# Up-projection of a decoder MLP: grouping the wide and the narrow products of a k-tile

## The chip, the cores and the metric

The kernel runs on one core of one Trainium2 chip. The metric is the device time of one execution in microseconds; for runs of the same kernel the median is taken. TensorE does the matrix products, VectorE (DVE) and ScalarE (ACT) prepare the weights and empty the accumulators, and the DMA queues of SyncE bring the weights from the chip's memory.

## The reference

Two consecutive decoder layers work on 256 tokens of width 2048, in float32. Each has a mixer (mLSTM heads and sliding-window attention) and an MLP with a squared ReLU; both are wrapped in RMSNorms whose shift, scale and gate come from a projection of a conditioning vector. The change is in the first product of the MLP:

```python
def squared_relu_mlp(h, w_up, w_down):
    return jnp.square(jax.nn.relu(h @ w_up)) @ w_down

def reference(...):
    for l in range(DEPTH):
        ...
        y = token_mixer(h, ...)
        x = x + gate_a * rms_norm(y, g_post_mix[l])
        h = rms_norm(x, g_pre_mlp[l]) * (1.0 + scale_m) + shift_m
        y = squared_relu_mlp(h, w_up[l], w_down[l])   # 2048 -> 8192 -> 2048
        x = x + gate_m * rms_norm(y, g_post_mlp[l])
```

## The kernel before

**Products in two parts.** Each float32 operand is split into a high part, rounded to the fp32r format, and a low part, the remainder, so that a product of two operands is made of three fp32r products: high x high, low x high and high x low. Weights arrive in tiles `raw` of 128 x 2048; `split` (line 227) makes from each half of such a tile a slab of two k-tiles: `whi` on ACT (L236) and `wlo` on DVE (L240). Four slabs of each kind are held, and `prefill` splits up to three ahead. In layer 0 and part of layer 1 DVE also works through the conditioning weights (`ada_op`, L208).

**Units.** A `Unit` is one block of 512 output columns over all its k-tiles of 128. `Unit.mm` calls its body once for each k-tile of a slab. There are several bodies:

- `body_xs` (L336) makes tokens the rows of the result: the weights stream past, 512 columns in each product. It is used for the down-projection (`dn`), the mixer's output (`op`) and up unit 0.
- `body_ws` (L341) makes weight columns the rows: the 256 tokens stream past, 256 columns in each product (`qa`, `qm`, `km`, and some up units).
- `body_wide` (L347) does the same for most up units, but streams the high and low tokens together: one product of 512 columns (`whi` with high and low tokens, L352) and one of 256 (`wlo` with the high tokens, L353). Each of the four groups of 128 weight columns has a PSUM bank of its own, `u.ps[j]`; the first half of the bank takes high x high and low-weight x high, the second half high-weight x low tokens. The 512-column product of the first k-tile starts the accumulation of the bank, the 256-column product of the last k-tile ends it.

With `body_wide` go the up units 4 to 15 of layer 0 and 2 to 15 of layer 1: 26 units of 16 k-tiles, with 4 products of each kind in a k-tile. Every product has its own load of 128 x 128 weights into the array (PEld in the profile).

**Order of the MLP.** Units are done in an order written out by hand: for each e from 0 to 7, up unit 2e + 2, then the four down units (e, c), then up unit 2e + 3. For e = 7 there is no further up unit, so the down units (7, c) come straight after up unit 15. A down unit (e, c) has 8 k-tiles, the first four from up unit 2e and the other four from 2e + 1.

**Banks.** There are two pools of four PSUM banks. Up units with an odd number (and unit 2) take the four banks of the pool `ps_x`, the others those of `ps_mm`; down units with c < 2 (from e = 1) take two of `ps_x`, the others two of `ps_mm`.

**Emptying.** `evac_up_wide` (L1056) goes over the four banks in two pairs. For a pair, ACT copies the second halves (L1063), DVE adds the first halves (L1065), after which the banks are free; then come the squared ReLU (L1068), the high part (L1069) and the low part (L1070) of the result, from which the down-projection reads.

**Order on the engines.** The instructions of an engine run in the order in which the program lists them. The framework that builds the program sorts instructions of one engine by priority and by what is ready by its own estimate, so that it can differ at single places from the order in which the code issues them.

Of the kernel before, what the change touches and what calls it, by code (L numbers as in the profile page):

```python
# [16 lines left out]
P = 128  # L17
D = 2048
KT = D // P
S = 256  # L20
# [19 lines left out]
def hymba_kernel(ctx: ExitStack, tc: tile.TileContext, x_d, c_d, cols_d, cons_d, wada_d,  # L40
                 wst_d, wsu_d, win_d, wg_d, wout_d, wup_d, wdn_d, out_d):
    nc = tc.nc
    V, A, T, G = nc.vector, nc.scalar, nc.tensor, nc.gpsimd
# [303 lines left out]
    def body_wide(u, xh, xl, wh, wl, kt):  # L347


        for j in range(4):  # L350
            cs = slice(j * P, (j + 1) * P)
            T.matmul(u.ps[j], wh[:, cs], u.act.both(kt), start=kt == 0, stop=False, skip_group_check=True)  # L352
            T.matmul(u.ps[j][:, 0:S], wl[:, cs], xh, start=False, stop=kt == u.nk - 1, skip_group_check=True)  # L353

    def body_mix(u, xh, xl, wh, wl, kt):
        for j in range(2):
# [183 lines left out]
    for l in range(DEPTH):  # L540
# [564 lines left out]
        def up(u):  # L1105

            un = Unit(f"up{L}_{u}", ("up", l, u), KT, hT2, body_wide, u % 2 == 1 or u == 2, 4)
            un.run()
            tups[u] = Task(evac_up_wide(un, u))
# [150 lines left out]
```

## Time and profile before

| | |
|---|---|
| time, median of 3 runs | 2243.57 us (2241.97 to 2245.36) |
| the profiled execution: time | 2245.62 us |
| the profiled execution: span | 2243.8 us |
| mean granted TensorE clock | 0.984 |
| TensorE busy (PE) | 2158.0 us, 96% |
| weight loads (PEld) | 1842.4 us, 82% |
| VectorE busy | 1719.7 us, 77% |
| ScalarE busy | 1097.5 us, 49% |
| mean DMA rate | 263 GB/s |

How to read it: each matmul row names its line and has the form output <- stationary or moving tiles, the array's rows and columns, the moving operand's shape, and the count. After the bar stand the total busy time, the mean duration of one instruction, and the idle time of the engine just before such instructions, with what ended it. Matmuls overlap each other in the array, so the duration of one is longer than the distance between the starts of two; the chain that ended last, in order of time, gives the distance. A line such as L333 belongs to a helper used by many units; the names of the tiles tell which unit it is (`up`, `dn`, `qa`).

### The profile page before, as it was taken

How to read it: one execution, taken by the hardware profiler on the slowest of the kernel's cores; microseconds unless marked ns; L12 is line 12 of the kernel's file. 1: busy time of each engine (PE TensorE's matmuls, PEld its weight loads, DVE VectorE, ACT ScalarE, POOL GpSimd, SP SyncE). 2: the span in 40 equal slices, each digit the busy share in tenths (PEclk: the TensorE clock that was granted, in tenths of full speed). 3: DMA queues.
4: the chain of work that ended last, by engine and by line, in shares of the span. 5: the costliest groups of instructions: out<-in, count | busy, mean ns of one | idle time of the engine just before them, and what ended most of it. 6: DMA issues, size and time to landing. Idle time of an engine off the chain costs nothing.

```text
span 2243.8 us, 29891 instructions
## 1 busy us (share of the span) xinstructions
PE 2158.0 (96%) x11658; PEld 1842.4 (82%) x11658; DVE 1719.7 (77%) x2386; ACT 1097.5 (49%) x1585; POOL 1.4 (0%) x14
## 2 busy tenths in 40 slices
PE   6789999899999999999989999989999999999998
PEld 5679777698888888888869988778888888888886
DVE  7989999688888888888577898957666767555557
ACT  4246753645444444434465566556443444444433
POOL 0000000000000000000000000000000000000000
PEclk9999999899999999999989999999999999999999
DMA  9998689498889888888539866745666667655551
GB/s 371 385 361 301 235 303 351 161 355 315 319 305 338 306 332 316 318 315 317 192 118 337 317 227 243 269 164 204 228 225 233 229 226 263 210 188 190 186 191 71
DMA packets 82351, 589.88 MB, mean 263 GB/s; under 512 B 9185, under 2 KB 9633, under 8 KB 10785
## 3 DMA queue, kind: packets, MB, share of 16 engines
q1 hardware_dynamic: 82210, 587.98, 71.7%
q8 instruction: 91, 1.49, 0.3%
q14 instruction: 50, 0.41, 0.1%
HBM read 585.81 MB, written 2.13 MB: 262 GB/s over the span
## 4 chain that ended last, share of the span: by engine, by line
PE 84%; DVE 10%; ACT 3%; issue 2%; DMA 1%; SPq 0%; DVEq 0%; ACTq 0%
PE dn L333 31%; PE up L352 17%; PE up L353 9%; PE up L333 6%; PE op L333 5%; DVE raw L208 4%; PE om L333 3%; PE vm L333 2%; PE qa L333 2%; DVE wlo L240 2%; PE qm L333 2%; PE km L333 2%; PE kva L333 1%; DVE x L400 1%; DMA raw<-in_wout_dram 1%
## 5 line engine op out<-in xcount | busy, mean ns | idle before, releaser
L240 DVE TENSOR_TENSOR wlo<-raw,whi 128x1024 fp32r<-128x1024 f32 x720 | 875.8, 1222 | 433.0 <-ACT whi L236 431.3
L236 ACT ACTIVATE whi<-raw 128x1024 fp32r<-128x1024 f32 x720 | 759.3, 1059 | 872.3 <-PE dn L333 344.2
L352 PE MATMUL up<-htm,whi 128*128 128x512 f32 x1664 | 588.3, 399 | 0.0
L353 PE MATMUL up<-htm,wlo 128*128 128x256 f32 x1664 | 467.5, 281 | 0.0
L208 DVE SCALAR_TENSOR_TENSOR raw<-raw,cact 128x2048 f32<-128x2048 f32 x192 | 437.2, 2284 | 7.1 <-DMA raw<-in_wada_dram 7.1
L333 PE MATMUL dn<-whi,sh 128*128 128x512 f32 x1024 | 399.5, 390 | 0.0
L333 PE MATMUL dn<-wlo,sh 128*128 128x512 f32 x1024 | 399.0, 390 | 0.0
L333 PE MATMUL dn<-whi,sl 128*128 128x512 f32 x1024 | 398.9, 390 | 0.0
L352 PEld LDWEIGHTS up<-htm,whi 128*128 128x128 f32 x1664 | 313.2, 188 | 77.1
L353 PEld LDWEIGHTS up<-htm,wlo 128*128 128x128 f32 x1664 | 314.6, 189 | 0.6
L333 PEld LDWEIGHTS dn<-whi,sh 128*128 128x128 f32 x1024 | 192.3, 188 | 40.6 <-DVE r L1065 0.4
L333 PEld LDWEIGHTS dn<-wlo,sh 128*128 128x128 f32 x1024 | 192.3, 188 | 40.2
L333 PEld LDWEIGHTS dn<-whi,sl 128*128 128x128 f32 x1024 | 192.4, 188 | 39.4 <-DVE sl L1087 0.2
L333 PE MATMUL op<-whi,ct 128*128 128x512 f32 x512 | 164.0, 401 | 2.6 <-ACT whi L236 1.8
L333 PE MATMUL vm<-whi,hta 128*128 128x512 f32 x256 | 90.9, 438 | 30.1 <-ACT whi L236 18.6
L333 PEld LDWEIGHTS op<-whi,ct 128*128 128x128 f32 x512 | 97.6, 192 | 25.2 <-ACT whi L236 2.7
L333 PE MATMUL op<-wlo,ct 128*128 128x512 f32 x256 | 101.3, 401 | 2.1 <-DVE wlo L240 2.0
L333 PE MATMUL qa<-hta,whi 128*128 128x256 f32 x512 | 93.6, 285 | 0.0
L333 PE MATMUL up<-htm,whi 128*128 128x256 f32 x512 | 92.8, 284 | 0.0
L333 PEld LDWEIGHTS vm<-whi,hta 128*128 128x128 f32 x256 | 51.5, 209 | 45.1 <-ACT whi L236 20.1
L333 PE MATMUL om<-whi,hta 128*128 128x512 f32 x256 | 82.3, 401 | 0.0
L333 PEld LDWEIGHTS up<-htm,whi 128*128 128x128 f32 x512 | 80.3, 192 | 0.5
(260 smaller groups left out, 2319.2 us busy)
## 6 DMA issues: line engine op xcount, KB each, us to landing
raw<-in_wada_dram SPq DMA_DIRECT2D x192, 1024.0 KB, 6.5
raw<-in_wdn_dram SPq DMA_DIRECT2D x128, 1024.0 KB, 4.9
raw<-in_wup_dram SPq DMA_DIRECT2D x120, 1024.0 KB, 5.1
raw<-in_win_dram SPq DMA_DIRECT2D x56, 1024.0 KB, 5.5
raw<-in_wout_dram SPq DMA_DIRECT2D x32, 1024.0 KB, 6.3
raw<-in_wst_dram SPq DMA_DIRECT2D x16, 1024.0 KB, 7.3
raw<-in_wsu_dram SPq DMA_DIRECT2D x8, 1024.0 KB, 6.3
gp<-gdr SPq DMA_DIRECT2D x4, 1024.0 KB, 5.7
```

What stands on the lines that cost most here:

```text
L208: V.scalar_tensor_tensor(w, w, 1.0, cact, ALU.mult, ALU.mult, accum_out=modc[l][:, v, j:j + 1])
L236: A.activation(hi, raw, AF.Copy)
L240: V.tensor_tensor(lo, raw, hi.bitcast(F32), ALU.subtract)
L333: T.matmul(o, a, w, start=not self.started[b], stop=last and i == 2, skip_group_check=True)
L352: T.matmul(u.ps[j], wh[:, cs], u.act.both(kt), start=kt == 0, stop=False, skip_group_check=True)
L353: T.matmul(u.ps[j][:, 0:S], wl[:, cs], xh, start=False, stop=kt == u.nk - 1, skip_group_check=True)
L400: V.scalar_tensor_tensor(xc, self.yg[c][tok], r, xc, ALU.mult, ALU.add)
```

## The change

In `body_wide` the loop over the four groups of weight columns is cut in two. The first loop does the four 512-column products of the k-tile, one in each of the four banks; the second does the four 256-column products, in the same order of the banks. The products themselves, their operands, their banks and their start and stop flags are the same. In the code before, the order in a k-tile was wide, narrow, wide, narrow and so on, the two of a bank directly behind each other.

```diff
     def body_wide(u, xh, xl, wh, wl, kt):
 
+        cs = [slice(j * P, (j + 1) * P) for j in range(4)]
         for j in range(4):
-            cs = slice(j * P, (j + 1) * P)
-            T.matmul(u.ps[j], wh[:, cs], u.act.both(kt), start=kt == 0, stop=False, skip_group_check=True)
-            T.matmul(u.ps[j][:, 0:S], wl[:, cs], xh, start=False, stop=kt == u.nk - 1, skip_group_check=True)
+            T.matmul(u.ps[j], wh[:, cs[j]], u.act.both(kt), start=kt == 0, stop=False, skip_group_check=True)
+        for j in range(4):
+            T.matmul(u.ps[j][:, 0:S], wl[:, cs[j]], xh, start=False, stop=kt == u.nk - 1, skip_group_check=True)
```

## The prediction, made before the changed kernel was built or run

> **What bounds the kernel now.** I read the page first: the engine shares, the chain that ended last, and the groups of the two lines that the change moves.
>
> ```profile
> PE 2158.0 (96%) x11658; PEld 1842.4 (82%) x11658; DVE 1719.7 (77%) x2386; ACT 1097.5 (49%) x1585; POOL 1.4 (0%) x14
> PE dn L333 31%; PE up L352 17%; PE up L353 9%; PE up L333 6%; PE op L333 5%; DVE raw L208 4%; PE om L333 3%; PE vm L333 2%; PE qa L333 2%; DVE wlo L240 2%; PE qm L333 2%; PE km L333 2%; PE kva L333 1%; DVE x L400 1%; DMA raw<-in_wout_dram 1%
> ...
> L352 PE MATMUL up<-htm,whi 128*128 128x512 f32 x1664 | 588.3, 399 | 0.0
> L353 PE MATMUL up<-htm,wlo 128*128 128x256 f32 x1664 | 467.5, 281 | 0.0
> ```
>
> TensorE bounds the kernel. The two moved lines carry 17% and 9% of the chain, about 580 us. Their idle time is 0.0, so nothing that they wait for can be saved: only their pace, or a new wait, can move the time. The mean durations (399 and 281 ns) are no price, because neighbours overlap; the price is the distance from one start to the next. Next, busy time by stage, for two units of up-projection in layer 1 (the window, its length, busy us of PE, PEld, DVE, ACT and POOL, the granted clock, DMA share and GB/s).
>
> ```profile
> 1633.60:1678.40 44.80, 44.80 (x256) 38.89 (x255) 27.65 (x29) 20.31 (x25) 0.00 (x0) 1.00 0.67 233
> ```
>
> PE is busy for the whole stretch at a granted clock of 1.00; DVE, ACT and the DMA have room. Last, the chain in order of time, for the pace of long runs and of the alternation.
>
> ```profile
> 1211.56 25.92 PE qa L333 x216
> 1590.03 43.58 PE dn L333 x192
> 1678.82 43.58 PE dn L333 x192
> ...
> 1640.31 0.23 PE up L352
> 1640.54 0.12 PE up L353
> ```
>
> The dn products stream 512 columns, the qa ones 256 (body_xs and body_ws). A run of 512-column products has one every 43.58 / 192 = 227 ns; a run of 256-column ones every 25.92 / 216 = 120 ns. A pair would be 347 ns at these paces. Between the two dn rows lie two up units, 2 x 64 pairs: (1678.82 - 1590.03 - 43.58) / 128 = 353.2 ns a pair. The alternation thus costs some 6 ns a pair more than the same work in long runs: that is all the change can win, 4 x 6.5 = 26 ns a k-tile, 10.8 us over 26 units x 16 k-tiles.
>
> **The change part by part.** *1. The pace.* Nothing is added or removed: 26 x 16 x 8 = 3328 matmuls, each with its weight load, change order on PE alone; no DMA and no instruction of another engine moves past a queue. A k-tile has 8 changes of width now and 2 afterwards, but a run of four is short. In layer 0, up unit 0 (512 columns, in runs of 12) and units 1 to 3 (256 columns, in runs of 72) take turns, and show how a run settles (256 columns up to 481.79, 512 from 481.91, 256 from 484.66; first column the start in us, x2 two neighbours of one line):
>
> ```profile
> 481.79 0.28 PE L333 MATMUL up<-htm,wlo 128*128 128x256 f32 x1
> 481.91 0.63 PE L333 MATMUL up<-whi,htm 128*128 128x512 f32 x2
> 482.38 0.39 PE L333 MATMUL up<-wlo,htm 128*128 128x512 f32 x1
> 482.61 0.62 PE L333 MATMUL up<-whi,htm 128*128 128x512 f32 x2
> 483.07 0.39 PE L333 MATMUL up<-wlo,htm 128*128 128x512 f32 x1
> ...
> 484.66 0.40 PE L333 MATMUL up<-htm,whi 128*128 128x256 f32 x2
> ...
> 485.01 0.40 PE L333 MATMUL up<-htm,whi 128*128 128x256 f32 x2
> ```
>
> The first three 512-column distances take 482.61 - 481.91 = 0.70 us, the next two 0.46, so four take 0.93 us against 4 x 0.227 = 0.908. Four 256-column ones take 485.01 - 484.66 + 0.12 = 0.47 us, a little under 0.48. A k-tile is then 1.40 us against 4 x 353.2 = 1.413. I take 1.401, a gain of 12 ns. It is the value nearest to the new pattern, since it is what a run of four does after a run of the other width. The bounds: 1.387 where a group settles at once (gain 26 ns), and, on the side of a loss, the 512-column products that follow an alternation:
>
> ```profile
> 1678.65 0.40 PE L333 MATMUL dn<-whi,sh 128*128 128x512 f32 x1
> ...
> 1679.60 0.39 PE L333 MATMUL dn<-whi,sl 128*128 128x512 f32 x1
> ...
> 1681.21 0.39 PE L333 MATMUL dn<-wlo,sh 128*128 128x512 f32 x1
> ```
>
> Here the first four take 1679.60 - 1678.65 = 0.95 us: 0.95 + 0.47 = 1.42 us a k-tile, 8 ns worse than now.
>
> One unit, the first of layer 0, already has the good pace:
>
> ```profile
> 575.90 0.23 PE up L352
> ...
> 579.72 0.23 PE up L352
> ```
>
> Eleven pairs in 3.82 us are 347 ns a pair, in the same order of instructions as elsewhere. The excess is thus no fixed price of a change of width; the pattern can lock in more than one way, which is why I keep both bounds. This unit would lose 16 x 14 ns = 0.2 us. The other 25 x 16 = 400 k-tiles gain 400 x 12 ns = 4.8 us.
>
> *2. Entering the down-projection.* After the alternation, eleven dn products take 1681.21 - 1678.65 = 2.56 us, against 11 x 0.227 = 2.497: 0.063 us lost. After a run of 256s five take 483.07 - 481.91 = 1.16 against 1.133, 0.027 lost. The difference, 0.036 us, at the 12 such places whose entry has no other wait: 0.4 us gained.
>
> *3. The end of a unit.* The four banks now finish 0.35 us apart; afterwards 0.12 us. Bank 0 is complete 0.70 us later relative to the unit's end. At two places, before the last down-projection of each layer (e = 7), the next unit takes exactly the banks that unit 15 just filled:
>
> ```profile
> 1103.45 0.28 PE L353 MATMUL up<-htm,wlo 128*128 128x256 f32 x1
> 1103.77 1.10 ACT L1063 ACTIVATE r<-up 128x256 f32<-128x256 f32 x3 [0.83 <-PE up L353]
> 1104.18 1.14 DVE L1065 TENSOR_TENSOR r<-up,r 128x256 f32<-128x256 f32 x3
> 1104.51 0.28 PE L353 MATMUL up<-htm,wlo 128*128 128x256 f32 x1
> 1104.66 0.19 PEld L333 LDWEIGHTS dn<-whi,sh 128*128 128x128 f32 x1 [0.19 <-DVE r L1065]
> ```
>
> The last product for bank 0 starts at 1103.45, then ACT copies, DVE adds, and only then the dn load starts. From that product to the unit's end it is 1104.63 - 1103.45 = 1.18 us now and 4 x 0.12 = 0.48 afterwards. The wait grows by 0.70 us, twice: 1.4 us lost. Behind the waiting load all of PE is queued. The other 24 unit ends have a whole up or down unit (48 x 0.227 = 10.9 us or more) before their banks or their result are needed, and PE's loads wait at none of them in layer 1's MLP, by the waits from its first unit to its last:
>
> ```profile
> PEld dn L333 <- DVE r L1065: 0.2, 1, 0.2
> ACT whi L236 <- PE up L352: 152.9, 89, 1.9
> ```
>
> ACT's first copy is later there too, by up to 0.70 us, with the splits of weights queued behind it. By the second row these splits wait 152.9 / 89 = 1.7 us each for PE to free a buffer, so ACT is ahead by more than it loses. That buffer is also freed 0.36 us earlier (4 x 0.12 instead of 0.12 before the slab's end), and the low half of the weights is needed 0.68 us later (after four 227 ns products instead of one). Neither ends a wait of PE; both cost nothing.
>
> *4. The start of the first wide unit in layer 0.* Its fourth bank is still being copied out:
>
> ```profile
> 572.16 0.39 PE L352 MATMUL up<-htm,whi 128*128 128x512 f32 x1
> ...
> 573.12 0.59 ACT L1114 ACTIVATE ys<-dn 128x512 f32<-128x512 f32 x1
> 573.56 0.71 PE L352 MATMUL up<-htm,whi 128*128 128x512 f32 x2
> ```
>
> The copy ends at 573.12 + 0.59 = 573.71; the build puts the fourth product off by a k-tile today, so that two 512-column ones (x2) stand in a row. In the new order it would be due at 572.16 + 3 x 0.227 = 572.84, so 0 to 0.9 us is lost, according to how far it is put off again. I take 0.3, nearer the low end, because the build moved it today.
>
> *Sum*: -4.8 + 0.2 - 0.4 + 1.4 + 0.3 = -3.3 us. The profiled execution took 2245.62 us (span 2243.8), so 2242.3 for it; it lies 2.0 above the median of the runs, 2243.57, and from that the forecast is 2240.3, 0.15% faster.
>
> **A rule of the skill.** The distance between products in the rows is 227 and 120 ns in runs, and 353 ns for a pair of both. The Trainium skill, "TensorE: Matmul & The Clock Gate", section "Back-to-back issue gap", makes an isolated gap N / 2.4 + 2.5 ns, whatever stands beside it; that estimate is 216 and 109 ns, 325 ns a pair in either order. By it the pace would gain nothing; the trace disagrees, with 353 against 347 ns for the same columns. It is the first rival below.
>
> **The rivals.** *The order is indifferent*: what a change of width costs grows with the length of the run, so that two changes with runs of four lose as much as eight with runs of one; or the build puts the products back into pairs, as it moved some at 573.56. For it: the longer runs do pay 0.02 us on settling. Against it: the rows at 481.91. Only terms 3 and 4 are left, 1.7 us: 2245.3, or 2243.6 with the pairs back. *The groups settle at once*, as the unit at 575.90 did: 400 x 26 ns = 10.4 us, with terms 2 to 4 (0.4 gained, 1.7 lost) 9.1 gained, 2234.5. For it: that unit lost nothing on four times as many changes of width. Against it: the 0.93 us. *The groups never settle*: four 512s take 0.95 us again and again as after the alternation. 400 x 8 ns = 3.2 us lost, with terms 3 and 4 (1.7) 4.9: 2248.5, slower. It decides from a k-tile of 1.413 + 0.007 us upwards. For it: the rows at 1678.65. Against it: those follow an alternation, which is no longer there.
>
> **How the numbers follow.** About 0.2% (4.5 us) is what a measurement of this kernel can tell from no change: faster means under 2239.1, slower over 2248.1. Forecast, 0.53: 2240.3, own range 2237.5 to 2243, of which 0.15 lies below 2239.1. Settling at once or nearly, 2234 to 2237.5: 0.20, all faster. Order indifferent: 0.17, all same. Never settling: 0.10, of which 0.08 slower. That is faster 0.35, same 0.57, slower 0.08. The range leaves out about a tenth at each end: 2235.5 to 2246.5.
>
> **What would show it.** In the changed kernel the chain between two dn rows should have eight products per k-tile in 1.40 us, (distance of two dn rows less 43.58) / 32. That is 44.8 us for two units, against 45.21. Within a k-tile the 512s should start 0.23 apart, the first ones more, and the 256s 0.12. PE's load of dn should wait on the DVE add about 0.9 us, once in each layer, and ACT's wait for the up product at L1063 should grow by 0.7 us a time. The prediction is wrong if a k-tile takes 1.387 or 1.42 us, if PE waits at other unit ends, or if the products stand in pairs again.

## The result and the profile after

| | before | after |
|---|---|---|
| median of the runs | 2243.65 us (2241.29 to 2246.63) | 2248.49 us (2240.55 to 2250.25) |
| ratio after / before | | 1.0015, 95% interval 1.0008 to 1.0021 |
| the profiled execution: time / span | 2245.62 / 2243.8 us | 2248.9 / 2247.1 us |

The changed kernel is slower by 0.15%. The forecast was 0.15% faster, and 2248.5 us lies above the range. The pace of the products became what was forecast, and its gain is in the trace; two places gave back more than it.

First the page of the changed kernel: shares of the engines, and the groups of the moved lines (L354 is the 256-column product now) and of the down-projection.

```profile
PE 2156.1 (96%) x11658; PEld 1842.7 (82%) x11658; DVE 1718.6 (76%) x2386; ACT 1093.2 (49%) x1585; POOL 1.4 (0%) x14
...
L352 PE MATMUL up<-htm,whi 128*128 128x512 f32 x1664 | 454.2, 394 | 0.0
L333 PE MATMUL dn<-whi,sh 128*128 128x512 f32 x1024 | 400.0, 391 | 4.5 <-DVE r L1066 4.5
L354 PE MATMUL up<-htm,wlo 128*128 128x256 f32 x1664 | 264.8, 281 | 0.0
```

PE is 1.9 us less busy while the span is 3.3 us longer. The moved lines still wait for nothing. The line that the change did not touch, the first product of the down-projection, now has 4.5 us of idle time ahead of it, put down to the DVE add that empties unit 15 (L1066 now, L1065 before).

The pace, from the chain in order of time in layer 1 (start, length, what, count):

```profile
1591.55 43.55 PE dn L333 x192
1679.97 43.57 PE dn L333 x192
...
1635.09 0.91 PE up L352 x4
1636.00 0.47 PE up L354 x4
1636.47 0.93 PE up L352 x4
1637.40 0.47 PE up L354 x4
```

Between two dn blocks lie two units of 16 k-tiles: (1679.97 - 1591.55 - 43.55) / 32 = 1.402 us a k-tile, where before it was 1.413 (4 x 353.2 ns); four wide products take 0.91 to 0.93 us, four narrow ones 0.47.

The entry of dn(7, 0) in layer 0, from the timeline; ahead of it stand unit 15's last narrow products (x4), and in the bracket is the idle time of the engine, of the weight load (PEld) and of the product (PE):

```profile
1101.73 0.63 PE L354 MATMUL up<-htm,wlo 128*128 128x256 f32 x4
...
1101.93 1.06 ACT L236 ACTIVATE whi<-raw 128x1024 fp32r<-128x1024 f32 x1 [1.75 <-PE up L352]
1102.90 1.19 ACT L1064 ACTIVATE r<-up 128x256 f32<-128x256 f32 x4
1103.02 1.23 DVE L240 TENSOR_TENSOR wlo<-raw,whi 128x1024 fp32r<-128x1024 f32 x1 [1.58 <-ACT whi L236]
1104.16 1.08 DVE L1066 TENSOR_TENSOR r<-up,r 128x256 f32<-128x256 f32 x3
...
1104.64 0.19 PEld L333 LDWEIGHTS dn<-whi,sh 128*128 128x128 f32 x1 [2.48 <-DVE r L1066]
1104.64 0.50 PE L333 MATMUL dn<-whi,sh 128*128 128x512 f32 x1 [2.27 <-DVE r L1066]
1104.97 0.39 PE L333 MATMUL dn<-whi,sl 128*128 128x512 f32 x1
...
1105.65 0.62 PE L333 MATMUL dn<-whi,sl 128*128 128x512 f32 x1
...
1106.07 0.63 PE L333 MATMUL dn<-wlo,sh 128*128 128x512 f32 x1
```

Read it from the end. PE waits 2.27 us, for the adds that start at 1104.16. DVE is late because it is busy with `wlo` until about then, and that `wlo` belongs to a split whose `whi` ACT began at 1101.93, ahead of unit 15's copies (1102.90). In the kernel before, three copies stood ahead of that split in ACT's queue: the copies start at 1103.77 (a row in the prediction), and the `whi` follows them:

```profile
1104.76 1.05 ACT L236 ACTIVATE whi<-raw 128x1024 fp32r<-128x1024 f32 x1
```

The order of the two queues has changed, though the diff touches neither engine. The last wide product, which frees the buffer for that split, is now issued before the first bank is complete; that the builder's sorting by readiness put the split first for this reason is inferred from the two orders.

The second reading is the spacing after the wait: 0.33 and 0.23 us first, then 0.42 us from 1105.65 on. The windows show why (window, its length, busy us of PE, PEld, DVE, ACT, POOL; the granted clock is the third number from the end). First the changed kernel in both layers, then the kernel before:

```profile
1105.50:1109.00 3.50, 3.50 (x10) 2.77 (x9) 2.66 (x5) 1.34 (x3) 0.00 (x0) 0.52 0.70 281
1109.00:1113.00 4.00, 4.00 (x19) 3.24 (x18) 1.28 (x2) 2.04 (x2) 0.00 (x0) 0.99 0.00 0
2191.50:2195.00 3.50, 3.50 (x11) 2.73 (x10) 2.54 (x5) 1.28 (x3) 0.00 (x0) 0.57 0.67 267
```

```profile
1105.50:1109.00 3.50, 3.50 (x17) 2.91 (x16) 3.47 (x6) 2.40 (x5) 0.00 (x0) 1.00 0.32 52
```

In 3.5 us there were 10 products against 17: the clock fell to about one half. The Trainium skill, "TensorE: Matmul & The Clock Gate", section "What's actually happening", lists these two clock states, with a release after some 3.4 us of sustained work; the length of the slow stretch here, 1105.65 to 1109.05 = 3.4 us, agrees. It puts the fall after an idle window of about 3.4 us, though, and here 2.27 us were enough.

The ledger, by the starts of the same products in both traces (after minus before):

| place | after - before | what happened since the line above |
|---|---|---|
| before the first wide unit | -0.86 us | (the executions differ here; nothing has changed yet) |
| first dn block after it | -0.54 | +0.32: the unit that already had the good pace |
| last dn block before unit 15, layer 0 | -2.25 | -1.71: pace, 10 units |
| first product of dn(7, 0) | -0.02 | +2.23: the wait, less unit 15's own gain of 0.16 |
| 6 us into it | +1.59 | +1.61: the clock, at half speed for 3.4 us |
| first wide units of layer 1 | +1.68 | +0.09 |
| last dn block before unit 15, layer 1 | -0.61 | -2.29: pace, 13 units |
| first product of dn(7, 0) | +1.61 | +2.22: the wait |
| 6 us into it, and to the end | +3.24 | +1.63: the clock |

Pace: 4.0 us won. The two entries: 2 x (2.22 + 1.62) = 7.7 us lost.

### The profile page after: what moved, and what is told of

Same layout as the page of the kernel before. It is cut to its first block, busy times and chain, and to the rows that moved or that the text cites. A ratio compares the mean times of both kernels' runs of the same rounds, so it can differ in the third digit from the quotient of the medians.

```text
span 2247.1 us, 29890 instructions
## 1 busy us (share of the span) xinstructions
PE 2156.1 (96%) x11658; PEld 1842.7 (82%) x11658; DVE 1718.6 (76%) x2386; ACT 1093.2 (49%) x1585; POOL 1.4 (0%) x14
## 4 chain that ended last, share of the span: by engine, by line
PE 77%; DVE 4%; ACT 1%; issue 1%; DVEq 0%; ACTq 0%
PE dn L333 31%; PE up L352 17%; PE up L354 9%; PE up L333 6%; PE op L333 4%; PE vm L333 2%; PE qa L333 2%; PE om L333 2%; PE qm L333 1%; PE kva L333 1%; DVE wlo L240 1%; DVE x L401 1%; PE km L333 1%; PE pss L613 0%; ACT jkm L88 0%
## 5 line engine op out<-in xcount | busy, mean ns | idle before, releaser
L352 PE MATMUL up<-htm,whi 128*128 128x512 f32 x1664 | 454.2, 394 | 0.0
L352 PEld LDWEIGHTS up<-htm,whi 128*128 128x128 f32 x1664 | 285.3, 189 | 39.2 <-ACT ys L1115 0.4
L354 PEld LDWEIGHTS up<-htm,wlo 128*128 128x128 f32 x1664 | 255.3, 189 | 35.4
L354 PE MATMUL up<-htm,wlo 128*128 128x256 f32 x1664 | 264.8, 281 | 0.0
L333 PEld LDWEIGHTS up<-htm,whi 128*128 128x128 f32 x512 | 80.3, 192 | 0.5
```

Of the source, the lines that this page charges most:

```text
L333: T.matmul(o, a, w, start=not self.started[b], stop=last and i == 2, skip_group_check=True)
L352: T.matmul(u.ps[j], wh[:, cs[j]], u.act.both(kt), start=kt == 0, stop=False, skip_group_check=True)
L354: T.matmul(u.ps[j][:, 0:S], wl[:, cs[j]], xh, start=False, stop=kt == u.nk - 1, skip_group_check=True)
```

## The experiments

My theory after the first comparison: the pace is won everywhere, and all of the loss is at the entry of dn(7, 0), from the order of the ACT and DVE queues there and the fall of the clock after the wait. The rival: the wait is the banks' own, the 0.9 us of the prediction, and the rest comes from elsewhere.

**Unit 15 alone in the old order, all others in the new one.**

```diff
+        n = 1 if u.unit[2] == 15 else 4
+        for j0 in range(0, 4, n):
+            for j in range(j0, j0 + n):
+                wide(j)
+            for j in range(j0, j0 + n):
+                narrow(j)
```

> The new order in all wide units but unit 15 of each layer, which keeps the pairs. Theory (entry): the loss sits only where the last down-projection of a layer starts right behind unit 15; 3.85 us at each of the two places in the traces, while the other 24 units won 3.7 us together. Then PE's load of dn waits 0.2 us again at both places and the time is 2243.65 - 3.7 = 2240.0 us, faster than before by about 0.16%. Rival (spread): grouping costs something that the run-to-run spread of the changed kernel hides all over the kernel; then the time stays near 2248.

Measured: 2239.54 us (2237.33 to 2243.12), ratio 0.9982 (0.9973 to 0.9990). The load's wait is 0.2 us at both places again. The loss sits at unit 15; without the new order there, the change gives about the pace gain that was forecast.

**The reverse: only unit 15 in the new order** (the same edit with `n = 4 if u.unit[2] == 15 else 1`).

> The old order everywhere but in unit 15 of each layer, which is grouped: 2 of 26 units. Theory (entry): nearly the whole loss and none of the gain: 2 x 3.85 us less 2 x 0.16 us, 2243.65 + 7.4 = 2251.0 us where the clock falls at both places, 2247.5 where it falls at neither (2 x 2.1 us of wait alone). Rival (spread): 2 of 26 units change little, 2243 to 2245.

Measured: 2249.26 us (2244.76 to 2253.89), ratio 1.0023 (1.0014 to 1.0032). One unit of each layer is enough for the loss. The profile of this run holds a surprise, in the timeline and in the window behind the wait:

```profile
1106.44 0.50 PE L333 MATMUL dn<-whi,sh 128*128 128x512 f32 x1 [2.27 <-DVE r L1075]
1106.78 0.40 PE L333 MATMUL dn<-whi,sl 128*128 128x512 f32 x1
```

```profile
1107.00:1110.50 3.50, 3.50 (x17) 2.87 (x16) 3.04 (x7) 2.29 (x3) 0.00 (x0) 1.00 0.85 304
```

The wait is the same 2.27 us, but the clock stays at 1.00, at both places. I come back to this below.

**The emptying ahead of the split.** All units in the new order, but the split in question is listed behind the third of unit 15's four copies on ACT and behind the first square on DVE.

```diff
-                    A.activation(r[:, k, :], ps[2 * b + k][:, S:2 * S], AF.Copy)
+                    cp_ = A.activation(r[:, k, :], ps[2 * b + k][:, S:2 * S], AF.Copy)
+                    if (b, k) == (1, 0):
+                        marks['hi'] = cp_.ins
...
-                un.run()
+                if (e, c) == (7, 0):
+                    un.slabs(1)
+                    hold.update(marks)       # the next split is issued after these
+                    un.slabs(1)
+                    hold.update(hi=None, lo=None)
+                    un.slabs(2)
+                else:
+                    un.run()
```

> The new order everywhere; the split of the one slab that had moved ahead of the emptying of unit 15 (a copy on ACT, a subtraction on DVE) is queued behind it again. Theory (queue order): of the wait of 2.27 us, 0.9 is what the later banks cost (as the prediction had it) and 1.4 is the split in front of the copies and adds. The wait falls to 0.9 us at each place, the clock stays at 1.00 or nearly, and the time is 2243.65 - 3.7 + 2 x 0.7 = 2241.3 us. Rival (banks alone): the order of the queues is a by-product, the late banks cause the whole wait: 2.2 us of wait and 2248 us as now.

Measured: 2241.11 us (2239.3 to 2243.55), ratio 0.9988 (0.9979 to 0.9996). The timeline of the entry:

```profile
1102.39 1.21 ACT L1064 ACTIVATE r<-up 128x256 f32<-128x256 f32 x4 [1.86 <-PE up L354]
1102.81 1.09 DVE L1068 TENSOR_TENSOR r<-up,r 128x256 f32<-128x256 f32 x3 [1.02 <-ACT r L1064]
...
1103.29 0.50 PE L333 MATMUL dn<-whi,sh 128*128 128x512 f32 x1 [0.58 <-DVE r L1068]
1103.47 1.08 ACT L236 ACTIVATE whi<-raw 128x1024 fp32r<-128x1024 f32 x1
```

With the copies first, `whi` comes at 1103.47 and PE waits 0.58 us by the product's row, 0.78 by its weight load's. The banks alone thus cost about what the prediction said; the other 1.7 us of the 2.27 were the queue order.

**Work in the wait.** The changed kernel, with ten extra 512-column products into a free bank ahead of dn(7, 0); they add work that the reference does not have.

```diff
+                if e == 7:
+                    fill = ps_mm.tile([P, 512], F32, tag="mm", name=f"fill{L}")
+                    for _ in range(10):
+                        T.matmul(fill, hT2(0)[0][:, 0:P], hT2.both(0), start=True, stop=True)
```

> The new order everywhere; ten more 512-column products, whose result nobody reads, are put on PE between unit 15 and the last down-projection of each layer, where PE stood idle for 2.27 us. Theory (clock): the idle time let the granted clock fall to about half for 3.4 us, which costs 1.6 us more at each place. With the filler the wait is covered (10 x 0.227 = 2.27 us), the clock in the first 4 us of dn is 1.00, its products are 227 ns apart from the start, and the time is 2248.5 - 3.2 = 2245.3 us. Rival (no clock): the slow products have another cause, such as their weights: they stay at 420 ns, 2248.5 us.

Measured: 2244.12 us (2241.17 to 2246.75), ratio 1.0000 (0.9992 to 1.0009). Against the changed kernel's 1.0015 that is 0.15%, or 3.4 us, for useless products. The timeline, and the window behind the gap:

```profile
1100.74 2.47 PE L1141 MATMUL fill<-htm 128*128 128x512 f32 x10
1103.17 0.50 PE L333 MATMUL dn<-whi,sh 128*128 128x512 f32 x1
```

```profile
1103.00:1106.00 3.00, 3.00 (x13) 2.33 (x13) 2.97 (x7) 1.16 (x2) 0.00 (x0) 1.00 0.76 210
```

The dn product starts no earlier after unit 15 than in the changed kernel, but the ones behind it keep 0.23 us: 13 of them in 3.0 us, at a clock of 1.00. So the fall of the clock is a cost of its own, beside the wait, and it does not come when PE has work in the gap.

**The changed kernel once more**, for its clock.

> The changed kernel once more, for another look at its two waits at the entry of dn(7, 0). Queue theory: the order of the instructions on each engine is fixed, so the wait is again 2.2 to 2.4 us at both places. Clock: if the fall of the granted clock after the wait depended on the wait's length alone, it falls again at both places and the dn products after it are 420 ns apart for about 3.4 us, with a span of 2246 to 2248 us; if it also depends on where the wait falls, one or none of the two places shows it and the span is 1.6 or 3.2 us shorter.

Measured: 2247.51 us, span 2245.7.

```profile
1103.03 0.50 PE L333 MATMUL dn<-whi,sh 128*128 128x512 f32 x1 [2.27 <-DVE r L1066]
...
1104.40 0.63 PE L333 MATMUL dn<-wlo,sh 128*128 128x512 f32 x1
```

The clock fell again, at both places (0.58 in the window 2190 to 2193.5). The span is 0.3 us under what was expected; this execution was ahead of the other by 1.6 us when the changed units began (the same product of the first MLP starts at 479.43 against 481.06). Three profiles, the same wait of 2.27 us: two with falls, one without. The length of the wait does not decide alone.

The traces show what does. Narrow windows find the instant of a change of the clock. In the first profile of the changed kernel it fell at 1105.65 and 2191.08, 1085.43 us apart, while the waits are 1085.87 apart; in the second at 1104.11 and 2189.54, again 1085.43 apart, while the waits are 1086.15 apart. So the falls do not keep a distance from the wait. They keep a grid: 1085.43 is 318 steps of 3.413 us, the length of one slow stretch. In the run with only unit 15 in the new order, which has no fall at its waits, the grid is given by two falls elsewhere, at 1153.77 and 1508.75 (104 steps apart); 14 steps before the first is 1105.98, in the middle of the wait from 1104.17 to 1106.44. First the changed kernel, the step ahead of the fall and the fall; then the other run, a fall that gives the grid and the two steps that share the wait:

```profile
1102.23:1105.65 3.42, 1.15 (x6) 0.86 (x5) 2.63 (x5) 1.85 (x5) 0.00 (x0) 1.00 0.31 81
1105.55:1105.64 0.09, 0.09 (x2) 0.06 (x1) 0.09 (x1) 0.00 (x0) 0.00 (x0) 1.00 0.00 0
1105.66:1105.75 0.09, 0.09 (x2) 0.09 (x1) 0.09 (x1) 0.00 (x0) 0.00 (x0) 0.50 0.00 0
```

```profile
1153.60:1153.76 0.16, 0.00 (x0) 0.00 (x0) 0.12 (x2) 0.16 (x1) 0.00 (x0) 1.00 0.00 0
1153.78:1153.90 0.12, 0.00 (x0) 0.00 (x0) 0.08 (x2) 0.12 (x1) 0.00 (x0) 0.50 0.00 0
1102.57:1105.98 3.41, 1.60 (x10) 1.22 (x8) 1.83 (x3) 2.15 (x5) 0.00 (x0) 1.00 0.59 250
1105.98:1109.39 3.41, 2.95 (x13) 2.44 (x14) 3.30 (x8) 1.28 (x3) 0.00 (x0) 1.00 0.63 211
```

A step in which PE was busy for 1.15 us of 3.42 was followed by a slow one; when a boundary cut the same wait in two, leaving 1.60 and 2.95 us, neither step was. The entry in layer 1 agrees: 1.14 us ahead of the fall at 2191.08, and 2.83 and 1.72 us where the wait is cut at 2191.42 and the clock stays. So in these six waits it is the place of the wait on this grid that decides, and the grid lies otherwise in each execution. The Trainium skill, "TensorE: Matmul & The Clock Gate", section "What's actually happening", calls the window of its activity monitor "free-running"; the grid in these traces agrees. The grid would also explain why the changed kernel spreads over 9.7 us and the kernel before over 5.3, since an execution would lose 1.6 us at none, one or both places; that is not shown here.

**Other banks for dn(7, c).** The wait can also go by its cause: down units (7, 0) and (7, 3) take the free pool, (7, 1) and (7, 2) the banks of unit 15. First with the new order, then with the old one.

```diff
-            return Unit(f"dn{L}_{e}_{c}", ("dn", l, (e, c)), 8, hs, body_xs, e > 0 and c < 2)
+            return Unit(f"dn{L}_{e}_{c}", ("dn", l, (e, c)), 8, hs, body_xs, c in (1, 2) if e == 7 else e > 0 and c < 2)
```

> The new order everywhere, unit 15 too; the down units of e = 7 take other banks: c = 0 and 3 those of the pool that is free, c = 1 and 2 those of unit 15, so that the first one need not wait for unit 15 to be emptied. Theory (entry): the wait at the first product goes; the products of k-tile 4, which read unit 15's result, come 24 x 0.227 = 5.45 us later, about when that result is ready (5.1 to 5.9 us after the unit's end in the trace), so 0 to 0.7 us is waited there. Clock 1.00. 2239.5 to 2241. Rival (the result, not the banks, is late): the wait of 2.3 us turns up again at k-tile 4 and the clock falls there: 2246 to 2248.

> The kernel before with the same exchange of banks for e = 7. Theory (entry): its wait of 0.2 us at each place goes, 0.4 us in all, which is less than can be measured: 2243.8 us. Rival (banks matter otherwise): a change of more than 2 us.

Measured: 2240.35 us (2236.96 to 2242.46), ratio 0.9981 (0.9972 to 0.9990) with the new order; 2243.7 us (2241.93 to 2245.65), ratio 0.9997 (0.9988 to 1.0006) with the old one. PE's load waits of the first, in both MLPs:

```profile
PEld dn L333 <- DVE sl L1071: 0.6, 2, 0.3
```

The wait of 2.27 us is gone, and what it had covered comes up: the down unit reads the second pair of unit 15's result at its seventh k-tile, and the low part (L1071) is late there: 0.3 us of wait for the load, 0.17 us in the distances of the products (0.29 and 0.34 us in the place of 0.23 twice). The same change of banks gives nothing measurable to the kernel before, so its effect is on the wait, not on the pace.

**Other groupings.** If four of a kind settle better than one, what do two, and eight? Two wide, then two narrow, twice in a k-tile (unit 15 in pairs):

```diff
+        n = 1 if u.unit[2] == 15 else 2
```

> As the run with unit 15 in pairs, but the other 24 wide units go two 512-column products, two 256-column ones, and so on: 4 changes of width in a k-tile instead of 2 (in groups of four) or 8 (in pairs). Theory (settling): what a round trip of widths costs above 227 and 120 ns a product grows with the run, but less than in proportion: 6.5 ns for runs of one, 16 for four. For two it should be 7 to 12 ns, two round trips a k-tile: 1.401 to 1.411 us a k-tile, 2239.5 to 2243.5. Rival (fixed price for each change of width): 16 ns for each round trip as in groups of four, 1.387 + 2 x 0.016 = 1.419 us, 2246.

Measured: 2234.78 us (2232.82 to 2238.35), ratio 0.9963 (0.9949 to 0.9976), beyond what either theory gave. Then eight wide and eight narrow products of a slab of two k-tiles (unit 15 in pairs):

```diff
+        for k in range(2):
+            for j in range(4):
+                T.matmul(u.ps[j], hi[:, k, cs[j]], u.act.both(kt0 + k), ...)
+        for k in range(2):
+            for j in range(4):
+                T.matmul(u.ps[j][:, 0:S], lo[:, k, cs[j]], u.act(kt0 + k)[0], ...)
```

> Unit 15 in pairs; the other 24 wide units take both k-tiles of a slab together: eight 512-column products, then eight 256-column ones, so one round trip of widths for two k-tiles. Theory (settling): the 12 and 72 products of up units 0 to 3 pay 20 ns a round trip, so a run of eight pays at most that: 1.387 + 0.010 = 1.397 us a k-tile against 1.403 in groups of four, 24 x 16 x 6 ns = 2.3 us less than the run with groups of four and unit 15 in pairs (2239.5): 2237.2 us. Rival (settling has no end): each further 512-column product costs as much more as the first four (23 ns in four), 8 of them 46 ns less 7: 1.406 us, no gain, 2240 to 2241 us.

Measured: 2238.37 us (2236.59 to 2240.75), ratio 0.9977 (0.9967 to 0.9986). The chains in order of time, two by two first, then the slab groups:

```profile
1583.26 43.55 PE dn L333 x192
1671.38 43.53 PE dn L333 x192
```

```profile
1586.24 43.55 PE dn L336 x192
1674.45 43.55 PE dn L336 x192
```

By the same working as above, a k-tile takes 1.393 and 1.396 us. Runs of one, two, four and eight give 1.413, 1.393, 1.402 and 1.396: not a price per change of width (two by two has four changes in a k-tile, the changed kernel two), and not one that grows or falls with the length of a run. My picture of settling, which had been right for four and eight, falls with two.

**The alternation, started otherwise.** The first unit of layer 0 had 347 ns a pair in the old order. What set it apart was its start: the build put off its fourth wide product, so that two wide products stood in a row (the prediction's row at 573.56). So: the old order everywhere, but the first k-tile of each wide unit two by two.

```diff
+        n = 2 if kt == 0 else 1
```

> The order of the kernel before (wide, narrow, by turns), but in the first k-tile of each wide unit two wide, two narrow, two wide, two narrow. Theory A (the alternation has two patterns that hold themselves, 346.7 ns a pair as in the first wide unit of layer 0 and 353.2 as elsewhere, and the two wide products at that unit's start set it into the quick one): k-tiles of about 1.387 us, 26 ns less than before over 25 units x 16, about 10 us: 2233.5 to 2236 us. Theory B (the pace follows from the grouping of the neighbouring products alone, and the first unit had it for another reason): k-tiles of 1.412 us but for the first of each unit, 0 to 0.5 us won: 2243 to 2244 us.

Measured: 2233.8 us (2231.63 to 2236.02), ratio 0.9953 (0.9939 to 0.9967), as theory A has it. The chain, and the timeline inside a unit, far behind its first k-tile:

```profile
1583.28 43.54 PE dn L333 x192
1671.20 43.53 PE dn L333 x192
```

```profile
1639.83 0.40 PE L353 MATMUL up<-htm,whi 128*128 128x512 f32 x1
1640.06 0.28 PE L356 MATMUL up<-htm,wlo 128*128 128x256 f32 x1
1640.18 0.39 PE L353 MATMUL up<-htm,whi 128*128 128x512 f32 x1
```

A pair takes (1671.20 - 1583.28 - 43.54) / 128 = 346.7 ns in the same alternation that takes 353.2 ns in the kernel before. In 24 of the 26 wide units the exchange at the start goes with the quick pace for the k-tiles behind it. It does not compel it. In this trace the first wide unit of layer 1, which no down unit precedes, is back at the old pace from its second k-tile on, and so is unit 10 of layer 1 behind a small product of another kind (L384) that comes in after its second k-tile; the trace of the seeded pairs with the other banks, below, has the same two. And in the run with only unit 15 in the new order, the first unit of layer 0 has the same two wide products in a row as in the kernel before, and yet the old pace. The chains, first of the first wide unit of layer 1 in the seeded kernel, then of the first unit of layer 0 in that other run:

```profile
1562.07 0.23 PE up L353
...
1568.79 0.24 PE up L353
```

```profile
573.99 0.24 PE up L353
...
580.00 0.23 PE up L353
```

That is 19 pairs in 6.72 us and 17 in 6.01, 354 ns a pair. So the same order can run at either pace, and what tips it is not known. From the start of the first MLP to its end the seeded trace wins 4.8 us on the kernel before, in the second 5.4.

**Combinations**, to see whether banks and pace add: two by two in all wide units with the other banks, and the seeded pairs with the other banks.

> All wide units in the order of two wide, then two narrow products; the down units of e = 7 take the banks that unit 15 did not just fill. Theory (the pace is set by the grouping, the entry by the banks and the queues, and the two add): k-tiles at 1.393 us as with two by two before, so 24 units win about 7.5 us over the pairs; unit 15 is won too (2 x 16 x 19.8 ns = 0.6 us) and the two entry waits of the kernel before (2 x 0.19 us) are gone: 2234.8 - 0.6 - 0.4 = 2233.8, range 2232.5 to 2236 us, no idle time of PE over 0.3 us at the entry of dn(7, 0) and a granted clock of 0.98 or more there. Rival (a wait comes back later, at the first k-tile that reads unit 15's result, because the emptying is now the last thing before it): 0.7 us and more at each place, 2235.5 us and above, and with a fall of the clock 2239.

> The seeded pairs (two wide, two narrow, by twos, in the first k-tile of each wide unit, pairs after that) together with other banks for two of the down units of e = 7. Theory (both are independent): k-tiles at 1.387 us as in the seeded kernel alone, and the entry waits of 0.2 us at the two places gone: 2233.8 - 0.4 = 2233.4 us, range 2232 to 2235. Rival (what the banks spare at the entry comes back at the first k-tile that reads unit 15's result, as 0.1 us did with two by two): 2233.6 to 2234 us, which can't be told from the seeded kernel alone. Were the pattern set by the way in which a unit is entered and not by its seed, the change of banks would leave the pace as it is, since all entries but those two are the same; a pace other than 1.387 us would speak against the seed.

Measured: 2235.28 us (2234.32 to 2237.45), ratio 0.9960 (0.9947 to 0.9972), and 2235.19 us (2232.31 to 2236.5), ratio 0.9962 (0.9948 to 0.9975). The paces are again 1.393 and 1.387 us. In the second no load of dn waits in the MLPs; in the first one waits in each, as its rival had it, though shorter:

```profile
PEld dn L333 <- DVE sl L1080: 0.6, 2, 0.3
```

That is the 0.2 us of the old entry, back at the seventh k-tile, where the load waits 0.3 us for unit 15's last low part and the products lose 0.17 us. The times cannot be told from those without the banks (0.9963 and 0.9953); a gain of 0.4 to 1 us, as was expected, lies below what these runs resolve. The simplest of the fastest kernels is the seeded one, 0.47% faster than the kernel before.

## Why the prediction was wrong, and where it was right

- *The pace (term 1) was right*: 1.401 us a k-tile forecast, 1.402 measured; 4.8 us forecast, 4.0 in the ledger and 0.16 in each unit 15, so 4.3. The rivals "order indifferent", "settle at once" and "never settle" are excluded by 1.402 for this kernel. That the time came out at the 2248.5 us of "never settle" is chance: that rival needs k-tiles of 1.42 us. That the rows of another stage (481.91 to 485.01) gave it, with units in which nothing of the order was alike but the runs of widths, was partly luck: the same picture would have put two by two between 1.401 and 1.411, and it took 1.393.
- *The first unit of layer 0 (0.2) and its start (0.3)*: forecast 0.5 lost, 0.32 measured, both together.
- *Entering the other down units (term 2)*: 0.4 forecast; no entry of its own stands out in the ledger, whose pace lines contain it.
- *The end of unit 15 (term 3) is the step that failed.* It took the right place, the right mechanism for the banks, and a size of 0.70 us more. Measured: 2.3 us more by the load's rows (2.48 against 0.19), 2.4 by the ledger with unit 15's own gain put back, and 1.6 us more for the clock: 4.0 in all at each place. The premise that failed stands in term 1: "no DMA and no instruction of another engine moves past a queue". A split did move, ahead of unit 15's copies on ACT and of its adds on DVE. The prediction saw that the split's buffer is freed 0.36 us earlier, but weighed it only for the other 24 unit ends, where it did cost nothing: PE's loads waited at none of them. At the two ends of e = 7 it counted only the later bank. It had asked whether a *late* split would stop PE; the harm came from an *early* one. With the split held back, PE waited 0.58 us by the product's row, 0.78 by its load's, against the 0.9 forecast: the part of term 3 that was thought through was right.
- *A sign that did not come.* ACT's wait for the up product ahead of the first copy was to grow by 0.7 us a time. Before, it came 26 times, 21.4 us in all; in the changed kernel the copies wait for no up product at all. The split had overtaken them at every wide unit's end, and it cost PE something at two.
- *The fall of the clock* was in no part of the prediction. The mean over the whole span, 0.98 in both kernels, hides it, and whether it comes depends on where the wait falls on the grid, which differs from one execution to the next.
- With term 3 at its measured size the prediction's sum is -4.8 + 0.2 - 0.4 + 8.0 + 0.3 = +3.3 us. The ledger has +4.1 from the first wide unit to the end (3.24 + 0.86); the rest is mainly that terms 1 and 2 together won 4.3 us and not 5.2.
- Left open: why the products have more than one pace for the same mixture, and what tips a unit into one or the other.

## What to carry to other kernels

When an edit moves the instruction that frees a buffer, look up what work that buffer's release lets in, and which urgent instruction stands behind it in the same in-order queue: earlier is not free where the builder sorts by readiness. Price a wait of TensorE of some two microseconds at its length plus a possible slow stretch behind it (here 1.6 us), and read the granted clock in windows of a few microseconds, not as a mean. Before reordering a whole loop for its pace, look whether one unit already runs the old order faster, and ask what differs at its start: here that small difference was worth more than the whole change.

## What the runs showed of the hardware

- Four wide and four narrow products of a k-tile took 1.413, 1.402, 1.396, 1.393 or 1.387 us, by their order and by how the unit began, all at a granted clock of 1.00 and without a wait. The alternation runs at 353.2 or 346.7 ns a pair over many k-tiles. With two by two in the first k-tile, 24 of 26 units ran at the second; units with the same order were seen at either.
- The granted clock changed on a grid of 3.413 us, which lies otherwise in each execution. A step in which PE was busy for a third was followed by one step at half the clock, which cost 1.6 us; steps busy for 47% and 50% were not. So a wait of 2.27 us brought the fall when it lay within one step (four places in two traces), 0.4 to 1.1 us after the work had begun again, and did not when a boundary cut it (two places in a third). With ten products in the gap it did not fall either.
